# Retention's key and query products ahead of its value products, and where its rotations stand

## The chip, the core and the metric

The kernel runs on one core of a Trainium2 chip. Each engine works through a queue of its own in order: TensorE (PE) multiplies, VectorE (DVE), ScalarE (ACT) and GpSimd (POOL) do the elementwise work, SyncE (SP) issues nearly all DMAs. The metric is the time of one execution in device microseconds.

## What is computed

A trunk of two layers for 1024 tokens of width 1024. Layer 0 has two branches, a diagonal state-space layer with a gated output and multi-scale retention with 8 heads; layer 1 is a convolution module. The change lies in layer 0. Of the reference this matters:

```python
# state-space branch: y comes out of the scan
y = jax.nn.gelu(y)
y = y * jax.nn.sigmoid(y @ glu_w + glu_b)
# retention: 8 heads, keys and queries 64 wide, values 128 wide
q = rope(q, positions) * (RET_DK ** -0.5)
k = rope(k, positions)            # [x1*cos - x2*sin, x1*sin + x2*cos]
scores = einsum('bnihd,bnjhd->bnhij', qc, kc) * intra        # within a chunk
kv = einsum('bnjhd,jh,bnjhe->bnhde', kc, k_dec, vc)          # into the state
# the state is carried over the chunks with a decay; out = intra + q * state,
# then every head is normalised by its own mean and variance
```

## The kernel before

Every float32 product is made of three products of split operands: `wh` (or `xh`) is a cast on ACT, `wl` (or `xl`) the remainder, a subtraction on DVE or POOL. `wnext` hands out weights in the order of a list (`plan`) two ahead of use: a load on SP, a cast on ACT, a subtraction. `weight_low` makes remainders of layer 1's weights early and stores them in DRAM: load `lf`, cast `lh` on ACT, subtraction, store `lo`. 24 such lows are made in layer 0; the constants `K_LOWS`, `V_LOWS` and `H_LOWS` say how many in which stretch, the argument `bufs` how many buffers each tile has.

The keys and queries of all heads, and the values, are each made by seven products of quarter sums in place of eight (Strassen's scheme): `ret_values` runs the value products V in the order `V_ORDER`, then `ret_keys` the key and query products K in the order `K_ORDER`. One product is 48 matmuls of 128x128 by 128x512. The first of all, V2, stands in front of the last output of the scan (`s5_out(7)`). ACT and DVE bring the banks into the values `vt` or the accumulators `acc`. Meanwhile `y_pass` applies the Gelu, and `y_operands` loads and splits y as operands `yh`, `yl` of the gated product.

Then come the heads, in four pairs (`ret_heads`): transposed keys (`ktp`, decayed into `kt`), key by value (`kv`), on DVE the chain of states `S`, the scores (`sp`, masked into `sc` on DVE), the output (`ro`), per head mean and variance (`mv`), the inverse root (`rs`: a square root on ACT that needs a table load, a reciprocal on DVE), the normalised output (`on`), its transposes (`rt`). Between these PE runs the gated product `mm_glu` of `glu_ahead`: a `tanh` on ACT, then on DVE a product with `yg`, which POOL has made of two loads.

The rotation (`ret_turn`): for keys and for queries, swapped copies `kswp`, `qswp` come by DMA, POOL multiplies the raw tile and the swapped one by the tables `ropek` in eight instructions, DVE adds in four. Pair 0's raw tiles stay in SBUF; those of pairs 1 to 3 are stored in halves to `kq_d` and loaded again, raw and swapped, beside the heads of the pair before.

The order on each queue is made by a scheduler at build time; `issue_after` keeps an instruction behind another in that order.

Of the kernel before, what the change touches and what calls it, by code (L numbers as in the profile page):

```python
# [19 lines left out]
P = 128  # L20
# [23 lines left out]
V_ORDER = (2, 3, 1, 4, 5, 6, 7)  # L44
K_ORDER = (1, 6, 7, 2, 5, 3, 4)
# [14 lines left out]
class Trunk:  # L60
# [22 lines left out]
    def plan(self):  # L83
# [4 lines left out]
        seq += [(None, f"V{i}_{j}") for i in V_ORDER for j in range(2)]  # L88
        seq += [(None, f"K{i}_{j}") for i in K_ORDER for j in range(2)]
# [86 lines left out]
    def wload_quarter(self, name):  # L176
# [3 lines left out]
        e = self.nc.vector if g == "V" and (i in (1, 2, 6) or j) else self.nc.gpsimd  # L180
# [165 lines left out]
    def layer0_front(self, st):  # L346
# [170 lines left out]
        self.v2 = self.value_product(2, xs[0][4:], [self.bank(f"mm_v2_{b}", aux=b == 3) for b in range(4)])  # L517
# [429 lines left out]
    def retention(self, st):  # L947
# [6 lines left out]
        nc.sync.dma_start(self.rk[:], A["rope_k"])  # L954
        self.mask = r0.tile([P, NH, P], F32, name="retmask")
        nc.sync.dma_start(self.mask[:], A["ret_mask"])
        self.g128 = r0.tile([P, 4], F32, name="g128")
        nc.sync.dma_start(self.g128[:], A["ret_g128"])
        self.kdec = r0.tile([P, NH, 64], F32, name="kdec")
        nc.sync.dma_start(self.kdec[:], A["ret_kdec"])  # L960
        self.reps = r0.tile([P, NH], F32, name="reteps")
        nc.sync.dma_start(self.reps[:], A["ret_eps"])
# [25 lines left out]
    def ret_turn(self, pair, raws=None):  # L988

        nc, tab, q = self.nc, self.rk, self.rq  # L990
        cs = [slice(h * HALF, (h + 1) * HALF) for h in range(2)]
        made = []
        for i, nm in enumerate("kq"):
            if raws:
                raw = src = raws[i]
            else:
                raw, src = q.tile([P, T], F32, name=f"{nm}raw_{pair}", tag="raw", bufs=2), self.kq_d[pair, i]
                nc.sync.dma_start(raw[:], src)
            swp = q.tile([P, T], F32, name=f"{nm}swp_{pair}", tag="swp", bufs=2)
            for b in range(4):  # L1000
                o = b ^ 1
                nc.sync.dma_start(swp[32 * b:32 * b + 32, :], src[32 * o:32 * o + 32, :])
            for c in cs:
                nc.gpsimd.tensor_tensor(raw[:, c], raw[:, c], tab[:, 0, c], op=ALU.mult)
            for c in cs:
                self.last_turn = nc.gpsimd.tensor_tensor(swp[:, c], swp[:, c], tab[:, 1, c], op=ALU.mult)
            made.append((nm, raw, swp))

        def finish():
            outs, adds = [], []  # L1010
            for nm, raw, swp in made:
                o = self.r0.tile([P, T], F32, name=f"{nm}rot_{pair}", tag=f"{nm}rot", bufs=1)
                outs.append(o)
                adds.append([lambda c=c, o=o, raw=raw, swp=swp: nc.vector.tensor_tensor(o[:, c], raw[:, c], swp[:, c], op=ALU.add)
                             for c in cs])
# [830 lines left out]
```

## Time and profile before

| what | value |
| --- | --- |
| median of 3 runs | 1180.71 us (1177.71 to 1185.98) |
| the profiled execution | 1179.18 us |
| its span | 1177.4 us |
| mean granted TensorE clock | 0.997 |
| PE busy | 1155.9 us, 98% |
| DVE busy | 954.2 us, 81% |
| POOL busy | 718.3 us, 61% |
| ACT busy | 566.6 us, 48% |
| value and key products on PE | about 336 to 496 us |
| heads with the gated product | about 496 to 645 us |

The span runs from the profiled execution's first instruction to its last; 1.8 us lie around it. PE's matmuls are pipelined and their ends are modelled, so that a matmul of 128x512 reads 0.39 us where the next starts 0.227 us later. The clock is the same in all slices, so times of PE's groups can be carried over.

### The profile page before, as it was taken

To read this page: it belongs to the slowest core of one execution; us is meant where nothing else is said; L and a number is where in the kernel's file an instruction comes from. 1 tells how busy PE (TensorE), PEld (TensorE's weight loads), DVE (VectorE), ACT (ScalarE), POOL (GpSimd) and SP (SyncE) were. 2 spreads that over 40 slices of the span, in tenths; PEclk is the share of its full clock that TensorE was granted. 3 is DMA by queue.
4 is the path that set the end of the run, shared out by engine and by line. 5 is a ranking of instruction groups with operands and counts; after the bars stand their busy time and mean duration, and the time that the engine had idled before them with its cause. 6 is when DMAs were issued, how large, how long until landed. Compare 5 with 4: busy or idle time off the path is not lost.

```text
span 1177.4 us, 17601 instructions
## 1 busy us (share of the span) xinstructions
PE 1155.9 (98%) x6102; PEld 958.2 (81%) x6102; DVE 954.2 (81%) x1541; ACT 566.6 (48%) x855; POOL 718.3 (61%) x499
## 2 busy tenths in 40 slices
PE   9999999999999999998999999999999999999997
PEld 7888788788887888877888788888888888888877
DVE  6889989999725666676888999579999999999643
ACT  7212342332236756413224846467756578544662
POOL 2049999888841143686532053439894689977742
PEclk9999999999999999999999999999999999999999
DMA  9359579877799979997676879975448653366863
GB/s 342 109 166 326 193 271 320 269 272 273 249 308 334 366 249 313 361 300 255 209 237 238 308 249 305 344 255 187 161 161 297 221 181 133 126 192 232 277 250 139
DMA packets 142137, 293.74 MB, mean 249 GB/s; under 512 B 14048, under 2 KB 42976, under 8 KB 141920
## 3 DMA queue, kind: packets, MB, share of 16 engines
q1 hardware_dynamic: 140896, 288.43, 72.2%
q10 hardware_dynamic: 1152, 4.19, 0.9%
q8 instruction: 48, 0.79, 0.3%
q14 instruction: 41, 0.34, 0.1%
HBM read 210.32 MB, written 81.20 MB: 248 GB/s over the span
## 4 chain that ended last, share of the span: by engine, by line
PE 70%; DVE 12%; DMA 10%; issue 3%; ACT 2%; SPq 1%; POOL 1%; DVEq 0%; ACTq 0%; POOLq 0%
PE mm_g L279 5%; PE mm_g L278 5%; PE mm_g L277 5%; PE mm_w L279 4%; PE mm_w L278 4%; PE mm_w L277 4%; PE mm_k L1026 4%; PE mm_a L279 2%; PE mm_b L278 2%; PE mm_a L278 2%; PE mm_b L279 2%; PE mm_a L277 2%; PE mm_b L277 2%; PE mm_oc L279 2%; PE mm_oc L278 2%
## 5 line engine op out<-in xcount | busy, mean ns | idle before, releaser
L1533 DVE SCALAR_TENSOR_TENSOR cv<-u,convw,cv 128x512 f32<-128x512 f32 x358 | 244.5, 748 | 4.5 <-ACT cv L1519 3.0
L1513 POOL TENSOR_TENSOR tp<-tp,tp 128x512 f32<-128x512 f32 x104 | 138.9, 1338 | 28.8 <-ACT tp L1512 23.5
L279 PE MATMUL mm_g<-xh,wl_g 128*128 128x512 f32 x256 | 100.8, 394 | 0.0
L278 PE MATMUL mm_g<-xl,wh_g 128*128 128x512 f32 x256 | 100.6, 393 | 0.0
L277 PE MATMUL mm_g<-xh,wh_g 128*128 128x512 f32 x256 | 100.4, 392 | 0.0
L1512 ACT ACTIVATE tp<-u,convw 128x512 f32<-128x512 f32 x104 | 69.8, 714 | 11.3 <-POOL tp L1513 11.0
L167 POOL TENSOR_TENSOR wl_K<-wf_K,wh_K 128x1024 fp32r<-128x1024 f32 x14 | 34.0, 2430 | 48.6 <-ACT wh_K L166 46.6
L278 PEld LDWEIGHTS mm_g<-xl,wh_g 128*128 128x128 f32 x256 | 48.1, 188 | 11.3 <-issue 1.6
L279 PEld LDWEIGHTS mm_g<-xh,wl_g 128*128 128x128 f32 x256 | 48.0, 188 | 10.5
L277 PEld LDWEIGHTS mm_g<-xh,wh_g 128*128 128x128 f32 x256 | 48.1, 188 | 9.6
L279 PE MATMUL mm_oc<-zh,wl_woc 128*128 128x512 f32 (+1 forms) x152 | 54.4, 359 | 0.6 <-DMA wl_woc<-lo_woc 0.6
L277 PE MATMUL mm_oc<-zh,wh_woc 128*128 128x512 f32 (+1 forms) x152 | 54.3, 361 | 0.0
L278 PE MATMUL mm_oc<-zl,wh_woc 128*128 128x512 f32 (+1 forms) x152 | 54.0, 356 | 0.0
L277 PE MATMUL mm_glu<-yh,wh_glu 128*128 128x512 f32 x128 | 51.2, 400 | 2.2 <-ACT yh L1270 2.2
L278 PE MATMUL mm_u<-xl,wh_u 128*128 128x512 f32 x128 | 50.0, 391 | 1.0 <-DVE xl L399 1.0
L278 PE MATMUL mm_glu<-yl,wh_glu 128*128 128x512 f32 x128 | 50.5, 394 | 0.2 <-DVE yl L1272 0.2
L279 PE MATMUL mm_glu<-yh,wl_glu 128*128 128x512 f32 x128 | 50.6, 396 | 0.0
L277 PE MATMUL mm_g<-h1h,wh_cg 128*128 128x512 f32 x128 | 50.3, 393 | 0.0
L277 PE MATMUL mm_a<-h1h,wh_ca 128*128 128x512 f32 x128 | 50.2, 392 | 0.0
L279 PE MATMUL mm_b<-h1h,wl_cb 128*128 128x512 f32 x128 | 50.2, 392 | 0.0
L279 PE MATMUL mm_a<-h1h,wl_ca 128*128 128x512 f32 x128 | 50.0, 390 | 0.0
L279 PE MATMUL mm_g<-h1h,wl_cg 128*128 128x512 f32 x128 | 49.8, 389 | 0.0
(834 smaller groups left out, 3671.9 us busy)
## 6 DMA issues: line engine op xcount, KB each, us to landing
wf_g<-w_ab SPq DMA_DIRECT2D x16, 512.0 KB, 6.2
a<-w_out SPq DMA_DIRECT2D x32, 256.0 KB, 4.5
ws<-a SPq DMA_DIRECT2D x32, 256.0 KB, 4.5
lf<-w_c SPq DMA_DIRECT2D x32, 256.0 KB, 5.1
wf_p<-ws SPq DMA_DIRECT2D x16, 512.0 KB, 4.8
wf_cb<-w_c SPq DMA_DIRECT2D x16, 512.0 KB, 5.0
wf_ca<-w_c SPq DMA_DIRECT2D x16, 512.0 KB, 4.8
wl_cb<-lo_cb SPq DMA_DIRECT2D x16, 512.0 KB, 3.3
```

Of the source, the lines that this page charges most:

```text
L167: e.tensor_tensor(wl[:].rearrange(fl), wf[:], wh[:].rearrange(fl).bitcast(F32), op=ALU.subtract)
L277: nc.tensor.matmul(ps, wh[:, kb, :], xh, start=start, stop=False, skip_group_check=chain)
L278: nc.tensor.matmul(ps, wh[:, kb, :], xl, start=False, stop=False, skip_group_check=chain)
L279: self.last_mm = nc.tensor.matmul(ps, wl[:, kb, :], xh, start=False, stop=stop, skip_group_check=chain)
L1026: self.last_mm = self.nc.tensor.matmul(ps, l[:, k, :], r[:], start=start and k == m == 0, stop=stop and k == 3 and m == 2, skip_group_chec ...
L1512: nc.scalar.mul(sk[:], u[:, k:k + HALF], cw[:, nb, k:k + 1])
L1513: gp.tensor_tensor(s0[:], s0[:], sk[:], op=ALU.add)
L1533: v.scalar_tensor_tensor(dst[:], *tap, accs_[i][:], op0=ALU.mult, op1=ALU.add)
```

## The change

The key products now run first: K2 takes V2's place in front of `s5_out(7)`, then the other six, then all seven value products. ACT copies and DVE adds the key products into accumulators; those of pairs 2 and 3 lie in the space of half the values. `turn` rotates in place, with swaps from SBUF to SBUF. Pair 2 and pair 0 (`TURNS`) are rotated during the values' sweep, pair 1 beside the heads of pair 0, pair 3 beside those of pair 2. Pair 2 (rotated) and pair 3 (raw) are stored and come back into the tiles of pairs 0 and 1 when these are done. All remainders of key and value weights are made on DVE. Of the 24 lows, 6 stand in the key sweep, 8 in the value sweep and 10 in the heads (before: 6 beside the values, 14 beside the keys, 4 in the heads). The y operands of the first half are made after V7, the second half after V5 and V3, and the gated product takes the first half first. Three weights of the projection after the heads are loaded behind the last load of `ys_d`. The core of the diff:

```diff
--- before.py
+++ after.py
-LOWS, K_LOWS, V_LOWS, H_LOWS = 24, 20, 6, (0, 2, 4, 4)
+LOWS, K_LOWS, V_LOWS, H_LOWS = 24, 6, 14, (0, 4, 8, 10)
 NG = 4
+TURNS = (2, 0)
...
-V_ORDER = (2, 3, 1, 4, 5, 6, 7)
-K_ORDER = (1, 6, 7, 2, 5, 3, 4)
+K_ORDER = (2, 3, 1, 4, 5, 6, 7)
+V_ORDER = (1, 6, 2, 7, 5, 3, 4)
...
-        self.nc.sync.dma_start(wf[:], src if len(src.shape) == 2 else src.rearrange("p k n -> p (k n)"))
+        with self.tc.issue_after(self.ys_loaded.ins) if name in ("p1_3", "p2_0", "p2_1") else nullcontext():
+            self.nc.sync.dma_start(wf[:], src if len(src.shape) == 2 else src.rearrange("p k n -> p (k n)"))
...
-        e = self.nc.vector if g == "V" and (i in (1, 2, 6) or j) else self.nc.gpsimd
+        e = self.nc.vector if True else self.nc.gpsimd
...
-        self.v2 = self.value_product(2, xs[0][4:], [self.bank(f"mm_v2_{b}", aux=b == 3) for b in range(4)])
+        self.k2 = self.key_product(2, xs[0][4:], [self.bank(f"mm_k2_{b}", aux=b == 3) for b in range(4)])
         self.s5_out(7)
...
+            self.ret_keys(vp)
             V = self.ret_values(vp)
-            raws = self.ret_keys(vp)
...
-        done = 0
-        cur = self.ret_turn(0, raws)
         self.glu_ahead(0)
         for pair in range(4):
-            K, Q, qadds = cur()
+            K, Q = self.kq[pair]
             with self.tc.issue_after((self.last_rs if pair else self.last_turn).ins):
-                for k in range(K_LOWS + H_LOWS[pair], K_LOWS + H_LOWS[pair + 1]) if pair < 3 else ():
+                for k in range(V_LOWS + H_LOWS[pair], V_LOWS + H_LOWS[pair + 1]) if pair < 3 else ():
                     self.weight_low(ry, k, (("la", "lb"), ("la", "lb")), 1, nc.gpsimd)
 
             def turned():
+                if pair in (0, 2) and pair + 1 not in TURNS:
+                    with self.tc.issue_after(self.last_kt.ins), self.tc.issue_after(self.last_yg.ins):
+                        self.turn(pair + 1)
...
-            if pair < 3:
-                cur = self.ret_turn(pair + 1)
-            self.ret_heads(pair, K, Q, qadds, V, turned)
+            self.ret_heads(pair, K, Q, V, turned)
+            if pair in (0, 1):
+                pl, tags, bufs = self.kq_home[pair]
+                self.kq[pair + 2] = [pl.tile([P, T], F32, name=f"{nm}rot_{pair + 2}", tag=t, bufs=bufs) for nm, t in zip("kq", tags)]
+                self.acc[pair + 2] = [t[:] for t in self.kq[pair + 2]]
+                for q in range(2):
+                    nc.sync.dma_start(self.kq[pair + 2][q][:], self.kq_d[pair + 2, q])
             if pair < NG - 1:
                 self.glu_ahead(pair + 1)
...
+    def turn(self, pair):
+
+        nc, tab = self.nc, self.rk
         cs = [slice(h * HALF, (h + 1) * HALF) for h in range(2)]
         for i, nm in enumerate("kq"):
+            raw = self.acc[pair][i]
+            swp = self.rq.tile([P, T], F32, name=f"{nm}swp_{pair}", tag="swp", bufs=2)
             for b in range(4):
                 o = b ^ 1
+                nc.sync.dma_start(swp[32 * b:32 * b + 32, :], raw[32 * o:32 * o + 32, :])
             for c in cs:
                 nc.gpsimd.tensor_tensor(raw[:, c], raw[:, c], tab[:, 0, c], op=ALU.mult)
             for c in cs:
+                nc.gpsimd.tensor_tensor(swp[:, c], swp[:, c], tab[:, 1, c], op=ALU.mult)
+            for c in cs:
+                self.last_turn = nc.vector.tensor_tensor(raw[:, c], raw[:, c], swp[:, c], op=ALU.add)
+            if pair > 1 and pair in TURNS:
+                nc.sync.dma_start(self.kq_d[pair, i], raw)
...
+    def key_product(self, i, xs, pss):
+
+        for j in range(2):
+            w = self.wnext(f"K{i}_{j}")
+            for b in (2 * j, 2 * j + 1):
+                self.part(pss[b][:], w, b, xs, start=i not in (6, 7), stop=True, chain=i in (1, 6, 7))
+        return pss
...
+        self.kq_home = [(self.rq, ("raw", "raw"), 2), (self.r0, ("krot", "qrot"), 1)]
+        self.kq = [[pl.tile([P, T], F32, name=f"{nm}rot_{p}", tag=t, bufs=bufs) for nm, t in zip("kq", tags)]
+                   for p, (pl, tags, bufs) in enumerate(self.kq_home)] + [None, None]
+        acc = self.acc = [[t[:] for t in self.kq[p]] for p in range(2)]
+        acc += [[self.vt[1][h][:, 2 * q:2 * q + 2, :].rearrange("p a n -> p (a n)") for q in range(2)] for h in range(2)]
...
+                for q, h in {2: ((0, 0),), 3: ((0, 1),), 4: ((1, 0),), 5: ((1, 1),)}.get(i, ()):
+                    self.last_copy = nc.scalar.copy(acc[b][q][:, h * HALF:(h + 1) * HALF], ps[:])
+                for q, h in {1: ((0, 0),), 5: ((0, 1),), 6: ((0, 1),), 7: ((1, 0), (1, 1))}.get(i, ()):
+                    c = slice(h * HALF, (h + 1) * HALF)
+                    self.last_add = v.tensor_tensor(acc[b][q][:, c], ps[:], acc[b][q][:, c], op=ALU.add)
...
+            pss = self.value_product(i, xs[i], held if i in (6, 7) else ps4)
+            if n == 0:
+                for p in range(2, 4):
+                    if p not in TURNS:
+                        for q in range(2):
+                            nc.sync.dma_start(self.kq_d[p, q], self.acc[p][q])
+            if n < len(TURNS):
+                self.turn(TURNS[n])
...
+            for h, kbs in {7: ((0, range(KB)),), 5: ((1, range(4)),), 3: ((1, range(4, KB)),)}.get(i, ()):
+                self.y_operands(vp, h, kbs)
...
-        for h in (0, 1) if nb else (1, 0):
+        for h in range(2):
...
-        with self.tc.issue_after(self.last_kt.ins):
-            for add in qadds:
-                add()
         turned()
```

How the queues stand before and now, at the three places of which the prediction speaks.

On DVE, in pair 0's heads, before, behind the transposed keys: pair 0's own query adds, two gated results, then the states `S` and the masks in a row; pair 1's key adds (`krot<-kraw,kswp`) come last.

```order
L1014 TENSOR_TENSOR qrot_4980<-qacc_4169,qswp_4898 128x512 x2
L1095 SCALAR_TENSOR_TENSOR yg_1_4913<-mm_glu_1_4918,yg_1_4913 128x512
L1095 SCALAR_TENSOR_TENSOR yg_0_4946<-mm_glu_0_4951,yg_0_4946 128x512
L1195 COPY S_5034<-kv_0_5035 128x128
L1197 SCALAR_TENSOR_TENSOR S_5034<-S_5034,g_3591,kv_0_5035 128x128 x3
L1197 SCALAR_TENSOR_TENSOR S_5034<-S_5034,g_3591,kv_0_5048 128x128 x2
L1210 TENSOR_TENSOR sc_0_5058<-sp_0_5060,retmask 128x512
L1197 SCALAR_TENSOR_TENSOR S_5034<-S_5034,g_3591,kv_0_5048 128x128
L1210 TENSOR_TENSOR sc_0_5059<-sp_0_5061,retmask 128x512
L1210 TENSOR_TENSOR sc_0_5058<-sp_0_5072,retmask 128x512
L1210 TENSOR_TENSOR sc_0_5059<-sp_0_5073,retmask 128x512
L1014 TENSOR_TENSOR krot_5292<-kraw_4997,kswp_4999 128x512 x2
```

Now: pair 1's adds (`krot_3597`, `qrot_3598`) stand between the transposed keys and the states, and within the states.

```order
L1169 TENSOR_TENSOR kt_4973<-ktp_0_4974,kdec 128x512
L1097 SCALAR_TENSOR_TENSOR yg_0_4881<-mm_glu_0_4886,yg_0_4881 128x512
L1169 TENSOR_TENSOR kt_4973<-ktp_0_4980,kdec 128x512
L1004 TENSOR_TENSOR krot_3597<-krot_3597,kswp_4986 128x512 x2
L1191 COPY S_5008<-kv_0_5009 128x128
L1097 SCALAR_TENSOR_TENSOR yg_1_4914<-mm_glu_1_4919,yg_1_4914 128x512
L1193 SCALAR_TENSOR_TENSOR S_5008<-S_5008,g_3589,kv_0_5009 128x128 x3
L1004 TENSOR_TENSOR qrot_3598<-qrot_3598,qswp_4997 128x512
L1193 SCALAR_TENSOR_TENSOR S_5008<-S_5008,g_3589,kv_0_5022 128x128
L1004 TENSOR_TENSOR qrot_3598<-qrot_3598,qswp_4997 128x512
L1193 SCALAR_TENSOR_TENSOR S_5008<-S_5008,g_3589,kv_0_5022 128x128 x2
L1206 TENSOR_TENSOR sc_0_5032<-sp_0_5034,retmask 128x512
```

What moved: four adds of the next pair, each of which waits for POOL, from behind the masks to between the links of `S`, on which the `ro` products wait.

On POOL, at the same place, before (the third gated weight's remainder, half of pair 1's rotation, two `yg`, a remainder, the first low):

```order
L269 TENSOR_TENSOR wl_glu_4909<-wf_glu_4907,wh_glu_4908 128x1024
L1004 TENSOR_TENSOR kraw_4997<-kraw_4997,ropek 128x512 x2
L1006 TENSOR_TENSOR kswp_4999<-kswp_4999,ropek 128x512 x2
L1091 TENSOR_TENSOR yg_1_4913<-yg_1_4913,yn_1_4915 128x512
L1091 TENSOR_TENSOR yg_0_4946<-yg_0_4946,yn_0_4948 128x512
L269 TENSOR_TENSOR wl_glu_5222<-wf_glu_5220,wh_glu_5221 128x1024
L234 TENSOR_TENSOR lh_4984<-lf_4983,lh_4984 128x512
L1004 TENSOR_TENSOR qraw_5008<-qraw_5008,ropek 128x512 x2
```

Now:

```order
L270 TENSOR_TENSOR wl_glu_4877<-wf_glu_4875,wh_glu_4876 128x1024
L1093 TENSOR_TENSOR yg_0_4881<-yg_0_4881,yn_0_4883 128x512
L1093 TENSOR_TENSOR yg_1_4914<-yg_1_4914,yn_1_4916 128x512
L1000 TENSOR_TENSOR krot_3597<-krot_3597,ropek 128x512 x2
L1002 TENSOR_TENSOR kswp_4986<-kswp_4986,ropek 128x512 x2
L1000 TENSOR_TENSOR qrot_3598<-qrot_3598,ropek 128x512 x2
L1002 TENSOR_TENSOR qswp_4997<-qswp_4997,ropek 128x512 x2
L235 TENSOR_TENSOR lh_4948<-lf_4947,lh_4948 128x512
```

What moved: all eight multiplications of pair 1's rotation (`x2` are two) stand behind the two `yg` products and ahead of the first low's subtraction.

On ACT, from the gated results of the second block to the square roots of pair 1, before:

```order
L1094 ACTIVATE mm_glu_1_5264<-mm_glu_1_5264,hgb 128x512
L1094 ACTIVATE mm_glu_0_5542<-mm_glu_0_5542,hgb 128x512
L233 CAST lh_5303<-lf_5302 128x512
L268 CAST wh_glu_5831<-wf_glu_5830 128x1024
L1094 ACTIVATE mm_glu_1_5575<-mm_glu_1_5575,hgb 128x512
L563 ACT_TABLE_LOAD
L563 ACTIVATE rs_0_5425<-mv_0_5416,reteps 128x4
L563 ACTIVATE rs_0_5443<-mv_0_5434,reteps 128x4
```

Now:

```order
L1096 ACTIVATE mm_glu_1_5242<-mm_glu_1_5242,hgb 128x512
L234 CAST lh_5271<-lf_5270 128x512
L1096 ACTIVATE mm_glu_0_5510<-mm_glu_0_5510,hgb 128x512
L234 CAST lh_5277<-lf_5276 128x512
L269 CAST wh_glu_5805<-wf_glu_5804 128x1024
L1096 ACTIVATE mm_glu_1_5543<-mm_glu_1_5543,hgb 128x512
L234 CAST lh_5283<-lf_5282 128x512
L234 CAST lh_5290<-lf_5289 128x512
L564 ACT_TABLE_LOAD
L564 ACTIVATE rs_0_5389<-mv_0_5380,reteps 128x4
L564 ACTIVATE rs_0_5407<-mv_0_5398,reteps 128x4
```

What moved: where one low's cast (`lh`) stood behind the `tanh` of pair 1's blocks and ahead of the table load for `rs`, there are four, each between or behind two `tanh`.

More of the change, by code (lines that the diff above doesn't have):

```diff
@@ L1005, in ret_turn @@
             for c in cs:
[L1006 to L1015, printed above, removed]
-            for add in adds[0]:
-                add()
-            return outs[0], outs[1], adds[1]
-        return finish
+                nc.gpsimd.tensor_tensor(swp[:, c], swp[:, c], tab[:, 1, c], op=ALU.mult)
[3 more added lines that the diff above has]
+                nc.sync.dma_start(self.kq_d[pair, i], raw)
     def part(self, ps, w, b, xs, start=False, stop=False, chain=False):
@@ L1106, in value_product @@
                     xh, xl = xs[2 * j + k]
-                    first, last = j == k == 0 and i not in (6, 7), j == k == 1
+                    first, last = j == k == 0 and i not in (6, 7, 3), j == k == 1
                     nc.tensor.matmul(pss[b][:], xh[:, o], wh[:, k, :], start=first, stop=False, skip_group_check=chain)
@@ L1132, in summed @@
             return v.scalar_tensor_tensor(o, ps, r, o, op0=ALU.mult, op1=ALU.add)
-        self.fetch = fetch
-        x12 = self.x12 = self.xs[1][:4]
-        spare = self.spare = [tuple(vp.tile([P, HALF], F32R, name=f"xt{q}{kb}") for q in "hl") for kb in range(4)]
-        xs = self.xq = {1: self.xs[0][:4], 2: self.xs[0][4:], 3: self.xs[1][4:], 4: fetch(4, x12), 5: fetch(1, spare)}
+        xs, self.ys_in, pss = self.xq, [[], []], {}
         for n, i in enumerate(V_ORDER):
+            if i in (1, 2, 5, 4):
+                ps4 = [self.bank(f"mm_v{i}_{b}", aux=i in (2, 5) or b == 3) for b in range(4)]
@@ L1139, in ret_values @@
             if i == 1:
-                held = pss = [self.bank(f"mm_v{i}_{b}") for b in range(4)]
-            elif i != 2:
-                pss = held if i in (6, 7) else [self.bank(f"mm_v{i}_{b}", aux=b == 3) for b in range(4)]
-            pss = self.v2 if i == 2 else self.value_product(i, xs[i], pss)
-            if i in (4, 5):
-                xs[{4: 6, 5: 7}[i]] = fetch(*{4: (2, x12), 5: (3, spare)}[i])
+                held = ps4
+            pss = self.value_product(i, xs[i], held if i in (6, 7) else ps4)
```

120 lines of the change are left out of this document (46 added, 74 removed).

## The prediction

> **What bounds the kernel now.** I read four views: the page's first two parts, the list of what TensorE (PE) waited for, the timelines of all engines around the heads of retention (496 to 650 us), and the groups by tile for the tiles that move. First the page (the second line is the span in 40 slices of 29.4 us).
>
> ```profile
> PE 1155.9 (98%) x6102; PEld 958.2 (81%) x6102; DVE 954.2 (81%) x1541; ACT 566.6 (48%) x855; POOL 718.3 (61%) x499
> DVE  6889989999725666676888999579999999999643
> ```
>
> PE is busy 98% of 1177.4 us and the change alters no matmul count, so only PE's waits can be gained, or new ones made. Here are those that lie in the changed stretch.
>
> ```profile
> PE rt L1260 <- DVE mv L1247: 2.4, 1, 2.4
> PE mm_glu L277 <- ACT yh L1270: 2.2, 1, 2.2
> PE rt L1260 <- DVE on L1252: 2.1, 2, 1.2
> PE mm_v L1108 <- ACT wh_V L166: 1.4, 1, 1.4
> ...
> PE kv L1187 <- DVE kt L1170: 1.0, 1, 1.0
> ...
> PE mm_glu L278 <- DVE yl L1272: 0.2, 1, 0.2
> ```
>
> Together 9.3 us: all that can be gained, under 1% of the time. After the heads PE waits for nothing worth 1 us, so a wait made or removed here moves the end one for one. What makes such a wait is seen in pair 0's heads. (Start, length, then the instruction; in brackets the idle time before it and what ended it.)
>
> ```profile
> 496.13 0.39 PE L277 MATMUL mm_glu<-yh,wh_glu 128*128 128x512 f32 x1
> 531.66 0.62 ACT L233 CAST lh<-lf 128x512 fp32r<-128x512 f32 x1 [9.88 <-DMA lf<-w_c]
> 532.30 1.28 ACT L563 ACT_TABLE_LOAD   x1
> 533.60 0.30 ACT L563 ACTIVATE rs<-mv,reteps 128x4 f32<-128x4 f32 x1
> 537.78 1.06 PE L1260 MATMUL rt<-ident,on 128*128 128x128 f32 x8 [2.37 <-DVE mv L1247]
> 539.81 0.61 ACT L233 CAST lh<-lf 128x512 fp32r<-128x512 f32 x1
> 547.99 0.62 ACT L233 CAST lh<-lf 128x512 fp32r<-128x512 f32 x1 [4.07 <-DMA lf<-w_c]
> 570.54 1.03 PE L1260 MATMUL rt<-ident,on 128*128 128x128 f32 x8
> ```
>
> The 2.37 us before pair 0's transposes (rt) are named after DVE, but ACT is late: its queue held a weight low's cast (lh) that waited 9.88 us for a load, and the square root (rs) stood behind it. From rs to rt passes 4.2 us (537.78 less 533.60). The lows share one buffer each way, so a low takes a whole cycle of load, cast, subtraction and store; the casts are 8.15 us apart (531.66, 539.81, 547.99). I call 496.13, the first gated matmul, T. Pair 1's transposes leave at T+74.4.
>
> **What is taken away.** If none of the six waits came back, 9.3 us go. For the 1.4 (wh_V behind the Gelus) I accept it: the key product's casts stand ahead of the Gelus on ACT now. For the 2.1 and 1.0 of pairs 2 and 3 too: 24 gated matmuls now lie between the two sets of transposes and 27 between the transposed keys and their product, where before nothing did, and at 0.227 us each (13 steps from 541.22 to 544.17) they are 5.4 and 6.1 us of cover.
>
> ```profile
> 541.22 0.39 PE L279 MATMUL mm_glu<-yh,wl_glu 128*128 128x512 f32 x1
> ...
> 544.17 0.39 PE L277 MATMUL mm_glu<-yh,wh_glu 128*128 128x512 f32 x1
> ```
>
> **The key and value sweeps.** Fourteen low parts of key weights go from POOL to DVE, with the value ones that POOL had.
>
> ```profile
> L167 POOL TENSOR_TENSOR wl_K<-wf_K,wh_K x14: 2392/2404/2721, 409.3 to 484.1; 128x1024 fp32r<-128x1024 f32 x14
> L167 DVE TENSOR_TENSOR wl_V<-wf_V,wh_V x10: 1208/1224/1696, 307.8 to 405.4; 128x1024 fp32r<-128x1024 f32 x10
> ```
>
> POOL loses 34 us and DVE takes 17, in slices where DVE is 5 to 6 tenths busy; each stands on DVE at least 4 us ahead of its first matmul, also where a rotation's add stands before it (pair 2's key adds are through early in the first value product). Cost 0; without that cover 1.2 us for each. The evictions of the seven key products move to ACT and DVE in the same number. One spot is tight: a bank of the second product waits for a copy that stands behind the landing of the last y_d store, by my walk free 1.6 us before PE needs it. I take 0, bound 1.5. The stores and loads of raw pairs fall from 18 to 8, which no PE wait names: 0. The projection's weights p1_3 are issued after the last ys load, some 17 us later, still 8 us ahead of their first matmul: 0.
>
> **Pair 1's rotation beside pair 0's heads.** This is the first large term. On POOL its eight multiplications now stand behind the third gated weight's low part and the two yg products; on DVE its four adds stand *inside* pair 0's state chain (S), and DVE works in order, so S, the masks and every product of S with the queries queue behind POOL.
>
> ```profile
> 507.98 0.62 ACT L1270 CAST yh<-yf 128x512 fp32r<-128x512 f32 x1 [5.40 <-DMA yf<-yn_d]
> 497.15 1.05 ACT L268 CAST wh_glu<-wf_glu 128x1024 fp32r<-128x1024 f32 x1
> 507.34 2.35 POOL L269 TENSOR_TENSOR wl_glu<-wf_glu,wh_glu 128x1024 fp32r<-128x1024 f32 x1
> 512.58 2.99 POOL L1006 TENSOR_TENSOR kswp<-kswp,ropek 128x512 f32<-128x512 f32 x2
> 515.53 2.97 POOL L1091 TENSOR_TENSOR yg<-yg,yn 128x512 f32<-128x512 f32 x2
> 501.10 3.37 POOL L1004 TENSOR_TENSOR qacc<-qacc,ropek 128x512 f32<-128x512 f32 x2 [0.64 <-DVE krot L1014]
> 528.23 2.52 POOL L1006 TENSOR_TENSOR qswp<-qswp,ropek 128x512 f32<-128x512 f32 x2 [0.18 <-issue]
> 521.92 0.34 DVE L1197 SCALAR_TENSOR_TENSOR S<-S,g,kv 128x128 f32<-128x128 f32 x1
> 523.16 0.27 PE L1232 MATMUL ro<-S,qrot 64*128 64x128 f32 x1
> ```
>
> The last y operand's cast came at T+11.9 before. It is now one product earlier in the program, but the loads still pass through three buffers of 5.4 us and a cast and a split each, so I put it at T+11.2 and the product's wait at 1 us in place of 2.4. Then in order: that cast 0.6, wh_glu 1.05, wl_glu 2.4, two yg 2.7, four pairs of rotation at 2.5 to 3.0, say 11: T+29.0. One DVE add of 0.7 and two S of 0.34: T+30.4. PE was at its first ro at T+27.0 (523.16), with 2.4 us of waits and 78 gated matmuls before it; now there are 68, so with the 1 us it is there at T+23.3. The wait is **7.1 us**; with rotations of 2.5 and a last cast 2 us earlier 4, with rotations of 3.4 about 10. The Trainium skill's page GPSIMD Engine Reference, section 1, Specifications, says that GpSimd shares its SBUF interfaces with VectorE and collides with its two-input instructions, which speaks against a rotation beside DVE's heads; the pairs here between 2.52 and 2.99 us agree with it, and by it the upper figures would hold.
>
> **Ten lows in the heads instead of four.** The second large term. H_LOWS puts four lows after pair 0's start, four after its last rs, two after pair 1's; still one buffer, subtracted by POOL. On ACT, pair 1's square root now stands behind the eighth. Low 1's subtraction stands behind the rotation on POOL: T+30.3. SP issues its store and then load 2: T+31.1.
>
> ```profile
> DMA to landing us min/median/max: 2.8/5.1/7.5
> ```
>
> Landed after 5.1 and cast: T+36.8. Six more cycles of 8.15 as measured: low 8 is cast at T+85.7. Table load 1.28 and 4.2 to the transposes: T+91.2. On the way the same queue holds pair 1's keys (their eviction stands on DVE behind a yg that waits for a tanh behind low 5: T+64.8, where PE could be at about 57) and its state (a yg behind low 6). These are inside the T+91.2, not added. Before, these transposes left at T+74.4: **+16.8 us**, the 7.1 in place of the old 2.4, 2.2, 0.9 and 0.2 included. Bounds: a landing of 2.8 makes a cycle of 5.4 (0.62 cast, 1.29 subtraction, 0.7 issue), low 8 comes at T+66.9, and PE's own T+68.7 (74.4 less waits of 5.7) plus 7.1 decides: +1.4. A landing of 6.5 makes 9.1 and T+98: +24. I take the measured cycle: same tiles, same buffers, same engines.
>
> **Pair 3's rotation beside pair 2's heads.** It is loaded raw, swapped in SBUF, turned, and its adds stand before pair 2's state on DVE.
>
> ```profile
> qraw<-kq_d SPq DMA_DIRECT2D x3, 512.0 KB, 7.9
> qswp<-kq_d SPq DMA_DIRECT2D x12, 128.0 KB, 7.8
> ```
>
> The query half: load 7.9, swap 7.8, rotation 5.0, add 1.4, state 2, one after the other. SP issues the load behind low 8's store, about T+88.5, so the state is there at T+112.6. From T+91.2 PE has 55 gated matmuls (12.5) and some 6 us of keys and scores: T+110. I take 2.5 us, bounds 0 and 9.
>
> **Sum.** 16.8 + 2.5, less 1.4 (wh_V), less 1.2 and 1.0 (second rt wait of pair 2, kv of pair 3): +15.7. On the profiled execution of 1179.18 (span 1177.4 and 1.8 around it) that is **1194.9 us**; against the median 1180.71 of the runs, which is 1.5 above the profiled one, +1.2%. 1% is about what a measurement of this kernel can tell from no change, since its three runs lie 0.7% apart.
>
> **Rivals.** (a) *The lows' loads land quickly* and their casts hold nothing. For it: the last low landed in about 2.9 us (its cast is at 547.99); against: its median is 5.1. Then 1.4 + 2.5 - 3.6: 1179.5. The skill's DMA: Bandwidth & Descriptors, section Anatomy of one DMA, fits 2.0 us plus bytes over 436 GB/s (measured on GpSimd's path); by it 256 KB would take an estimated 2.6 us and this rival would hold, but the trace's median of 5.1 contradicts it. (b) *The rotation is not in the way*: if the last y operand comes at T+3, POOL is through 8 us earlier, S waits for nothing and the lows start 8 us earlier: pair 1's transposes at T+83.2, +8.8, in all 1179.2 + 8.8 + 2.5 - 3.6 = 1186.9. Against: three buffers. (c) *Faster*: neither queue binds, all 9.3 us go: 1169.9. For it: no key or value product waits for DMA; against: pair 0's cast, which cost 2.4 us with only four lows. (d) *Pair 3's chain decides as well*: SP's queue holds its loads one low longer (8 us): 1194.9 + 6.5 = 1201.4, up to 1208. For it: 14 loads and swaps of it stand between stores that wait; against: PE then is late too.
>
> **Chances.** Forecast 0.52, (a) 0.18, (b) 0.09, (c) 0.05, (d) 0.16. Of the forecast's share three quarters lie over 1% (1192.5), with all of (d): slower 0.55. Faster by over 1% needs under 1168.9, thus more than (c): 0.03. Within 1%: 0.42. The range 1179 to 1208 reaches from (a) to the end of (d).
>
> **What would show it.** In the profile after: PE's waits headed by ro or S of pair 0 (5 to 11 us, behind POOL's rotation), rt of pair 1 behind lh and rs, with kv of pair 1 between; ten lh on POOL about 8 us apart; wh_V gone from the list. If the lows come 5 to 6 us apart, or ro of pair 0 waits under 3 us, I am wrong on that term. If the sweeps show waits of over 2 us, I missed one.

## The result, and the profile after

The changed kernel takes 1198.75 us (median of 5 runs, 1197.17 to 1199.80), the one before 1180.42 on the same chip (5 runs, 1177.71 to 1185.98): ratio 1.0153, 95% interval 1.0134 to 1.0171. It is slower by 1.5%. The profiled execution has a span of 1198.0 us, 20.6 more than before. What PE waited for, longest first (total, times, longest):

```profile
PE mm_w L278 <- ACT ysh L1293: 8.9, 1, 8.9
PE rt L1256 <- DVE mv L1243: 3.2, 1, 3.2
PE sp L1200 <- DVE S L1193: 3.0, 2, 1.9
PE ro L1228 <- DVE S L1193: 2.6, 1, 2.6
PE mm_w L280 <- DVE wl_p L168: 2.6, 1, 2.6
PE mm_v L1110 <- DVE v L1126: 2.2, 1, 2.2
```

Of the six waits shown before, those of wh_V, of the second transposes of pair 2, of kv and of yh and yl are gone. One is new and larger than any of them: the first product of the output projection (mm_w) waits 8.9 us for the split row block ysh. The timeline around it, PE, SP's issues and ACT:

```profile
649.27 1.03 PE L1256 MATMUL rt<-ident,on 128*128 128x128 f32 x8
650.63 0.92 SPq L1262 DMA_DIRECT2D yr_d<-grl  x2
654.58 0.80 SPq L1298 DMA_DIRECT2D yr<-yr_d  x2
655.42 0.43 SPq L1307 DMA_DIRECT2D t2f<-ys_d  x1
659.45 0.63 ACT L1293 ACTIVATE ysh<-t2f 128x512 fp32r<-128x512 f32 x1 [2.27 <-DMA t2f<-ys_d]
660.13 1.65 PE L278 MATMUL mm_w<-ysh,wh_p 128*128 128x512 f32 x3 [8.90 <-ACT ysh L1293]
```

From pair 3's last transposes to that product it takes 10.9 us: product with the gate, store, load of the gated rows (t2f), split. Before it took 13.4, and PE waited for nothing in between, since 55 of the 384 gated matmuls came behind those transposes. The two ends before:

```profile
631.73 1.03 PE L1260 MATMUL rt<-ident,on 128*128 128x128 f32 x8
645.09 0.62 PE L277 MATMUL mm_w<-ysh,wh_p 128*128 128x512 f32 x2
```

Now 380 gated matmuls stand ahead of the last transposes and 4 behind (counted in PE's order).

A second thing is seen in the granted clock. From 330 us to 1174 it is 0.50 in six stretches of the changed kernel and in one of the kernel before (last line), and 1.00 outside them (us; PE, PEld, DVE, ACT, POOL busy; granted clock; DMA):

```profile
474.44:477.84 3.40, 3.40 (x10) 2.62 (x9) 2.51 (x4) 0.59 (x2) 0.00 (x0) 0.50 0.90 301
522.23:525.62 3.39, 3.39 (x15) 2.32 (x15) 2.05 (x4) 0.34 (x1) 3.39 (x3) 0.50 0.88 239
573.43:576.82 3.39, 3.39 (x14) 2.90 (x12) 3.25 (x17) 1.30 (x4) 0.00 (x0) 0.50 0.78 201
597.32:600.72 3.40, 3.40 (x20) 3.18 (x17) 1.85 (x6) 0.00 (x0) 0.00 (x0) 0.50 1.01 356
655.35:665.57 10.22, 5.44 (x12) 3.93 (x13) 7.44 (x11) 4.68 (x8) 1.46 (x1) 0.50 0.96 325
754.34:757.73 3.39, 3.39 (x10) 2.62 (x9) 3.39 (x3) 2.15 (x4) 2.88 (x2) 0.50 0.83 219
508.71:512.10 3.39, 3.17 (x10) 2.29 (x11) 1.86 (x2) 1.38 (x2) 3.39 (x3) 0.50 0.75 222
```

Across the large wait the clock falls at 655.3 and stays at 0.50 until 665.6: matmuls of 512 columns start every 0.427 us there, and every 0.227 afterwards. A wait of this length is paid for twice.

**Where the 20.6 us are.** The span of each kernel's profiled execution, cut at the same events (us; *ratio* is the time against before on the same chip, with its 95% interval; *sweeps* from the first key or value product to the first gated matmul, *heads* to the last transposes, *gap* to the first mm_w):

| run | median | ratio | ahead | sweeps | heads | gap | rest |
|---|---|---|---|---|---|---|---|
| before | 1180.4 |  | 336.3 | 159.8 | 135.6 | 13.4 | 532.3 |
| changed | 1198.8 | 1.0153 (1.0134-1.0171) | 335.0 | 162.6 | 151.6 | 10.9 | 537.9 |
| ys_early | 1204.2 | 1.0215 (1.0188-1.0242) | 334.9 | 159.6 | 150.9 | 15.2 | 538.7 |
| weights_free | 1196.5 | 1.0147 (1.0128-1.0167) | 334.0 | 160.8 | 153.4 | 13.2 | 533.1 |
| lows_in_sweep | 1189.8 | 1.0100 (1.0071-1.0129) | 334.3 | 160.4 | 145.1 | 11.1 | 536.6 |
| lows_on_dve | 1200.2 | 1.0166 (1.0137-1.0195) | 335.7 | 161.2 | 156.4 | 10.8 | 534.7 |
| turn1_in_sweep | 1194.7 | 1.0139 (1.0116-1.0162) | 336.1 | 166.3 | 141.6 | 10.7 | 534.7 |
| gated_first | 1194.1 | 1.0121 (1.0098-1.0144) | 335.5 | 160.1 | 151.7 | 3.4 | 540.5 |
| gated_lows | 1185.7 | 1.0057 (1.0033-1.0081) | 335.2 | 160.1 | 146.7 | 3.4 | 538.4 |
| gated_lows_turn1 | 1186.5 | 1.0055 (1.0034-1.0077) | 336.0 | 166.4 | 139.2 | 3.4 | 540.2 |
| all_three | 1186.4 | 1.0060 (1.0041-1.0079) | 334.1 | 159.9 | 147.1 | 3.4 | 540.9 |
| no_lows_in_heads | 1192.0 | 1.0107 (1.0079-1.0135) | 333.9 | 160.5 | 152.0 | 2.1 | 541.4 |
| turn1_lows_early | 1187.2 | 1.0072 (1.0045-1.0098) | 334.9 | 168.4 | 137.3 | 3.4 | 541.0 |
| turns_in_sweep | 1190.5 | 1.0099 (1.0067-1.0132) | 332.8 | 171.7 | 138.6 | 1.9 | 541.6 |

Heads and gap together are 13.5 us longer. The waits there are 17.7 (8.9, 3.2, 3.0, 2.6) in place of 7.9 (2.4, 2.2, 2.1, 1.0, 0.2): 9.8. In the heads the clock is 0.50 for 10.2 us in place of 3.4; at half clock at most half of the time is lost, so at most 3.4 more. These two leave some 0.3. The rest is 5.6 longer: the wait for wl_p at 753 us (2.6, before 0.5) and at most 4.4 lost at half clock (5.4 us at 0.50 behind the 8.9, 3.4 behind that wait). The sweeps lose 2.8: a wait of 2.2 for a bank where the 1.4 of wh_V stood, and at most 1.7 of half clock behind it. What lies ahead of the sweeps gives 1.3 back.

Each row is one execution. What lies ahead of the sweeps is the same work in all thirteen changed versions and takes 332.8 to 336.1 us there, and sweeps with the same lows and rotations take 159.6 to 162.6. So a difference of up to 3 us in one column is not shown by one row; the waits and the clock behind it are.

### The profile page after: what moved, and what is told of

The parts are those of the page before. It is cut to its first block, busy times and chain, and to the rows that moved or that the text cites. A ratio compares the mean times of both kernels' runs of the same rounds, so it can differ in the third digit from the quotient of the medians.

```text
span 1198.0 us, 17558 instructions
## 1 busy us (share of the span) xinstructions
PE 1164.4 (97%) x6102; PEld 965.6 (81%) x6102; DVE 957.7 (80%) x1545; ACT 571.2 (48%) x863; POOL 691.0 (58%) x487
## 4 chain that ended last, share of the span: by engine, by line
PE 67%; DVE 11%; DMA 11%; issue 5%; POOL 3%; ACT 2%; SPq 1%; DVEq 0%; POOLq 0%; ACTq 0%
PE mm_k L1013 6%; PE mm_g L280 6%; PE mm_g L279 6%; PE mm_g L278 5%; PE mm_w L278 3%; PE mm_w L279 3%; PE mm_w L280 3%; PE mm_a L280 2%; PE mm_a L278 2%; PE mm_b L280 2%; PE mm_b L278 2%; PE mm_b L279 2%; PE mm_a L279 2%; PE mm_oc L280 2%; PE mm_oc L279 2%
## 5 line engine op out<-in xcount | busy, mean ns | idle before, releaser
L234 ACT CAST lh<-lf 128x512 fp32r<-128x512 f32 x32 | 19.9, 621 | 93.0 <-DMA lf<-w_c 92.8
L279 PEld LDWEIGHTS mm_g<-xl,wh_g 128*128 128x128 f32 x256 | 48.1, 188 | 11.2 <-issue 1.6
L1000 POOL TENSOR_TENSOR v<-v,ropek 128x512 f32<-128x512 f32 x4 | 6.1, 1540 | 84.2 <-DMA kswp<-v 78.1
```

The lines of the kernel that those rows point to most:

```text
L234: self.nc.scalar.copy(hi[:], f[:])
L279: nc.tensor.matmul(ps, wh[:, kb, :], xl, start=False, stop=False, skip_group_check=chain)
```

## The experiments

Medians and ratios as in the table. The runs were on other chips, where the kernel before took 1177.6 to 1180.0 us and not 1180.4. So the ratios compare versions better than the times do, and two versions whose intervals overlap widely are not told apart.

**ys_early.** The theory first read from the trace: the gated rows' loads are late because of their place in SP's queue.

```diff
-                self.ys_loaded = nc.sync.dma_start(sg[:], self.ys_d[rows(nb), hs(h)])
+                self.ys_loaded = nc.gpsimd.dma_start(sg[:], self.ys_d[rows(nb), hs(h)])
```

> The changed kernel with one thing else: the eight loads of the gated rows 0 to 3 from DRAM (t2f and t3f from ys_d, L1307) are issued by POOL behind its product yg of block (6,1), not by SP behind the two stores of pair 3's output (yr_d) and the loads yr that wait for them. Theory A (the order on SP makes the wait of 8.9 us in front of the first w_out product): these loads land some 15 us before they are needed, the wait of mm_w for ysh falls from 8.9 to 1 to 5 us (what is left is the tanh of the last gated blocks, which stands on ACT at 654.0 to 657.2 behind a table load), and the time is 1191 to 1195. Rival B (the wait belongs to pair 3's late transposes, whose result the w_out products need anyway): the wait moves to the products that read yr0, and the time stays at 1197 to 1200.

Measured 1204.24 us (1201.03 to 1206.62; 1.0215 of before, 1.0188 to 1.0242): slower than the changed kernel and than both theories said. Theory A is wrong. POOL's issue and what then stands ahead of the split on ACT:

```profile
650.09 0.71 POOL L1307 DMA_DIRECT2D t2f<-ys_d  x1 [19.33 <-DVE wl_p L168]
659.44 0.62 ACT L1266 CAST yr00h<-yr0f 128x512 fp32r<-128x512 f32 x1 [6.67 <-DMA yr0f<-yr_d]
659.96 0.62 ACT L1293 ACTIVATE ysh<-t2f 128x512 fp32r<-128x512 f32 x1
```

POOL was free for 19.3 us and still could not issue the load. The row names the DVE instruction that ended last before it, but the program's own semaphores say what was waited for: t2f_0 waits for DVE's last product into grl_7 and for stores to land, since the tiles t2f_0, t3f_0, t2f_1 and t3f_1 lie on the addresses of pair 3's tiles grl_7 and grl_6. On SP that wait was hidden in the order, since the store and a load behind it stood ahead. So whatever needs row 0 comes a store and a load behind the last transposes. The new queue made another order on ACT, where the split now stands behind the cast of a later load: 4.3 us more. Other tiles for these rows were not tried: beside the stage's other tiles 1.9 KB per partition are left, less than one tile.

**weights_free.**

```diff
-        with self.tc.issue_after(self.ys_loaded.ins) if name in ("p1_3", "p2_0", "p2_1") else nullcontext():
+        with nullcontext():
```

> The changed kernel without the one condition that holds the loads of the w_out weights p1_3, p2_0 and p2_1 back until the ys rows are loaded. Theory A (the loads of ys_d stand behind the stores of yr_d on SP, whatever the weights do): the wait of 8.9 us stays within 1 us and the time is 1197 to 1200. Rival W (the late weights are what the w_out products wait for): the time falls by 3 us or more, to 1190 to 1196.

Measured 1196.48 (1194.60 to 1196.78): between the two, 2.3 less than the changed kernel, but against before the ratio is 1.0147 for 1.0153, which is no difference. The wait for ysh grew to 11.2 and the one for wl_p at 753 went; the table's rest is 4.8 us shorter and heads and gap some 4 longer. So the condition is not the cause of the large wait, and that it is worth anything in all is not shown.

**lows_in_sweep.**

```diff
-LOWS, K_LOWS, V_LOWS, H_LOWS = 24, 6, 14, (0, 4, 8, 10)
+LOWS, K_LOWS, V_LOWS, H_LOWS = 24, 8, 20, (0, 2, 4, 4)
```

> The changed kernel with its lows placed as before in the heads: four of them beside the heads (0, 2, 2, 0 per pair) instead of ten, the other six in the two sweeps (8 of 24 in the keys', 20 by the end of the values'). Theory P (the prediction's largest term: ten lows on ACT and POOL delay the transposes of pair 1): pair 1's transposes come 8 us or more earlier and the time falls to 1185 to 1191. Theory T (read from the trace after: the lows ran in 7.0 us each and pair 1's transposes were only 1.6 us later than before, so the lows hardly cost anything): 1196 to 1200, and the wait in front of the first w_out product stays at 8 to 10 us, since the transposes of pair 3 still stand behind 380 of the 384 gated matmuls.

Measured 1189.82 (1187.75 to 1194.62), 8.9 less, some 6 by the ratios: theory P's time. T's time is wrong, though the last wait stays as T said. The heads are 6.5 us shorter, by fewer waits and by the clock (0.50 for 3.4 us of them in place of 10.2). The sweeps are no longer although they hold six lows more. What PE still waits for:

```profile
PE mm_w L278 <- ACT ysh L1293: 9.2, 1, 9.2
PE mm_w L280 <- DVE wl_p L168: 2.6, 2, 1.7
PE sp L1200 <- DVE S L1193: 2.0, 1, 2.0
PE mm_v L1110 <- DVE v L1126: 1.7, 1, 1.7
PE rt L1256 <- DVE mv L1243: 1.2, 1, 1.2
```

Pair 1's transposes leave 69.9 us behind the first gated matmul instead of 75.5, 5.6 earlier and not the 8 of P.

**lows_on_dve.**

```diff
-                    self.weight_low(ry, k, (("la", "lb"), ("la", "lb")), 1, nc.gpsimd)
+                    self.weight_low(ry, k, (("la", "lb"), ("la", "lb")), 1, nc.vector)
```

> The changed kernel with the subtraction of the ten lows beside the heads on DVE instead of POOL; their loads, casts and stores stay. It asks by what the ten lows cost 7 us in the heads (lows_in_sweep). Theory Q (by POOL: its queue holds yg and wl_glu back, and DVE's two-input operations are slowed while it works): the transposes of pair 1 come 3 us or more earlier and the time is 1190 to 1195. Rival D (by the casts on ACT and the load and store each low waits for, or 0.7 us more of DVE inside the heads' chains): 1197 to 1202.

Measured 1200.20 (1195.24 to 1201.54): rival D, though the ratio, 1.0166, is not clear of the changed kernel's. The heads are 4.8 us longer. A subtraction on DVE waits for its cast, and what comes behind it waits too; the clock is at 0.50 for 17.1 us of the heads in place of 10.2. One such row, and the wait for the state S (6.9 in two, 3.0 in the changed kernel):

```profile
565.17 0.69 DVE L235 TENSOR_TENSOR lh<-lf,lh 128x512 fp32r<-128x512 f32 x1 [6.25 <-ACT lh L234]
PE sp L1200 <- DVE S L1193: 6.9, 2, 3.8
```

So DVE is no better place than POOL. The lows' loads and casts on ACT are the same in both; what of their cost is these and what is POOL's queue, the runs don't separate.

**turn1_in_sweep.**

```diff
-TURNS = (2, 0)
+TURNS = (2, 0, 1)
```

> The changed kernel with the rotation of pair 1 also in the values' sweep (behind the third of its seven products), so that only pair 3's stands beside the heads. Theory R (the rotation's additions on DVE inside pair 0's chain, and its products on POOL, make the waits of 3.0 and 2.6 us in front of pair 0's scores and outputs): these two fall below 1.5 us together and the time is 1192 to 1196. Rival S (the sweep has no room: rotation, splits and evictions on DVE come late there): the waits of mm_v grow from 2.2 by as much as the heads win, and the time is 1197 to 1202.

Measured 1194.72 (1191.21 to 1195.78): theory R's time, but the ratio, 1.0139, is not clear of the changed kernel's. Pair 0's waits for S are gone and the heads are 10.0 us shorter, but rival S is right too: the sweeps are 3.7 longer than the changed kernel's, 5 to 7 longer than those of the other runs with two rotations there. First two of DVE's splits, one while POOL turns and one when it is done; then what PE waits for:

```profile
449.48 2.31 DVE L168 TENSOR_TENSOR wl_V<-wf_V,wh_V 128x1024 fp32r<-128x1024 f32 x1
450.67 3.99 POOL L1002 TENSOR_TENSOR qswp<-qswp,ropek 128x512 f32<-128x512 f32 x2
476.07 1.21 DVE L168 TENSOR_TENSOR wl_V<-wf_V,wh_V 128x1024 fp32r<-128x1024 f32 x1
478.09 0.77 PE L1110 MATMUL mm_v<-wh_V,xh 128*128 128x512 f32 x1 [3.92 <-DVE v L1126]
```

The same split takes 2.31 us beside POOL's product and 1.21 without it. At 474.2 DVE is still behind: an add of the rotation, a low, a y split and that wl_V stand ahead of the eviction v (477.20), for whose bank the sixth product waits. How much of this is the slower splits and how much the adds themselves, the runs don't separate.

**gated_first.** After ys_early the order of the sum is changed, not the load: the four row blocks that need no load come first.

```diff
-BLOCKS = ((4, 0), (4, 1), (0, 0), (0, 1), (1, 0), (1, 1), (5, 0), (5, 1), (2, 0), (2, 1), (3, 0), (3, 1), (6, 0), (7, 0), (6, 1), (7, 1))
+BLOCKS = ((4, 0), (4, 1), (5, 0), (5, 1), (6, 0), (7, 0), (0, 0), (0, 1), (1, 0), (1, 1), (2, 0), (2, 1), (3, 0), (3, 1), (6, 1), (7, 1))
...
-        for kb in range(KB):
-            self.mm3(ps, w, kb, (xs[kb][0][:], xs[kb][1][:]), first and kb == 0, kb == KB - 1, True)
+        for n, kb in enumerate((4, 5, 6, 7, 0, 1, 2, 3) if first else range(KB)):
+            self.mm3(ps, w, kb, (xs[kb][0][:], xs[kb][1][:]), first and n == 0, n == KB - 1, True)
```

> The changed kernel with another order in front of the w_out products: of the eight row blocks that the first four products sum, the four that were gated late (4 to 7, never stored) come first, and the four that are loaded from ys_d last; the loads and splits of rows 0 to 3 stand behind those of rows 4 to 7 in the code. Theory C (after ys_early: the tiles t2f_0, t3f_0, t2f_1, t3f_1 lie in the memory of pair 3's tiles grl, so their loads wait for its last products and stores wherever they are issued, and everything that needs row 0 begins 11 us behind the last transposes): the first products begin on row 4 some 5 to 7 us earlier, with 36 matmuls (8 us) to cover the loads, and the time is 1190 to 1194. Rival B (what follows needs pair 3's output as late anyway): the wait moves to the products that read rows 0 to 3 or yr0, and the time stays at 1196 to 1200.

Measured 1194.14 (1192.31 to 1195.29), 4.6 less, some 4 by the ratios, whose intervals just overlap: theory C, 0.1 over its upper end. The first product comes 3.4 us behind the last transposes instead of 10.9; 2.6 of the gain are lost again in the rest:

```profile
650.72 0.98 PE L278 MATMUL mm_w<-ysh,wh_p 128*128 128x512 f32 x3 [1.48 <-ACT ysh L1293]
659.70 0.62 ACT L1266 CAST yr00h<-yr0f 128x512 fp32r<-128x512 f32 x1 [4.83 <-DMA yr0f<-yr_d]
660.22 0.62 ACT L1293 ACTIVATE ysh<-sg 128x512 fp32r<-128x512 f32 x1
660.90 0.96 PE L278 MATMUL mm_w<-ysh,wh_p 128*128 128x512 f32 x3 [2.50 <-ACT ysh L1293]
```

Row 7's split, whose data are long there, stands on ACT behind the cast of a load that lands at 659.7.

**gated_lows**: gated_first and lows_in_sweep together.

> gated_first and lows_in_sweep together. Theory C with the lows' own cost: the two gains are at different places (the heads, and the wait behind them) and add up: 1189.8 less 5 to 7 is 1182 to 1186. Rival: with the lows gone from the heads the scheduler puts the gated products elsewhere and the tail wait is not shortened: 1188 to 1191.

Measured 1185.70 (1183.37 to 1190.94; 1.0057 of before, 1.0033 to 1.0081): the gains add, 13.1 us in all (11 by the ratios). With the next two it is the fastest version; the runs don't tell these three apart. In the table its sweeps are those of before, heads and gap 1.1 longer. What is left is in the rest: PE waits four times for operands of the output projection between 646 and 670 us, 4.2 us together, and the clock is at 0.50 from 647.2 to 650.6.

**gated_lows_turn1**: with `TURNS = (2, 0, 1)` too.

> gated_lows with pair 1's rotation in the values' sweep as well. If the gains add (turn1_in_sweep had 10 us less between the first gated matmul and the first w_out product than the changed kernel, and lost 6 of them in the sweep; lows_in_sweep had 6 less): 1178 to 1183, no slower than before. Rival (the sweep is full: 20 lows and three rotations on DVE and POOL there, where a subtraction on DVE takes 1.78 in place of 0.68 us while POOL works): mm_v and wl_V waits reach 8 us or more, and the time is 1185 to 1190.

Measured 1186.51 (1184.57 to 1187.26): the rival's time, with waits of 5.5 us (mm_v 4.8, wl_V 0.7) for its 8. The heads win 7.5 us, the sweeps lose 6.3, the rest 1.8.

**all_three**: gated_lows and weights_free together.

> gated_lows without the condition that holds the w_out weights p1_3, p2_0 and p2_1 back. In gated_lows the fourth product then waits 1.2 us for wh_p (ACT) and 1.7 for wl_p (DVE), 667.39 and 669.65. Theory W: with the wait for ysh out of the way these late weights are the next thing that is late, and the time falls by 2 to 4 us to 1181 to 1184. Rival: the earlier weights take DMA and ACT from the loads and splits of the ys rows, as in weights_free (wait 11.2 in place of 8.9): 1185 to 1189.

Measured 1186.44 (1183.89 to 1187.93): the rival's time; its reason is not shown. The waits in the fourth product are still there:

```profile
PE mm_w L278 <- ACT wh_p L167: 2.0, 1, 2.0
PE mm_w L280 <- DVE wl_p L168: 1.3, 1, 1.3
```

**no_lows_in_heads**: all_three with `24, 8, 24, (0, 0, 0, 0)`.

> all_three with no low beside the heads (8 in the keys' sweep, 16 in the values'). If the lows cost in proportion (ten cost 7 to 9 us against four), the last four are worth 3 to 5 us: 1177 to 1181, as long as the values' sweep holds 16; rival: the sweep is full, mm_v waits 3 us or more longer, and the time is 1183 to 1188.

Measured 1191.96 (1189.69 to 1194.30): slower than either said. The sweep is no longer (160.5), but its last lows reach into pair 0, where DVE waits for a cast and the transposed keys (kt) queue behind. The wait of 4.57 is paid for twice as well: the clock is at 0.50 from 516.0 to 529.7.

```profile
515.48 0.69 DVE L235 TENSOR_TENSOR lh<-lf,lh 128x512 fp32r<-128x512 f32 x1 [3.21 <-ACT lh L234]
516.82 3.26 PE L1183 MATMUL kv<-v,kt 128*64 128x128 f32 x28 [4.57 <-DVE kt L1169]
```

**turn1_lows_early**: all_three with `TURNS = (2, 0, 1)` and `24, 12, 20, (0, 2, 4, 4)`.

> all_three with pair 1's rotation in the values' sweep, and four more of the lows in the last two products of the keys' (12 there, 8 in the values'). It asks whether the 4.8 us of mm_v in gated_lows_turn1 come from the count of DVE operations in the sweep. Theory F (DVE is full there, lows and rotation alike): with four lows fewer mm_v waits under 2.5 us, and the time is 1178 to 1182. Rival: the wait stays at 4 to 5 us, since the eviction stands behind the splits of the y rows and of wl_V, which are as before: 1182 to 1186.

Measured 1187.18 (1185.44 to 1190.35): the rival's reading, 1 us over its range. With four lows fewer in the values' sweep the wait is longer, not shorter, so it does not hang on their count.

```profile
478.02 0.76 PE L1110 MATMUL mm_v<-wh_V,xh 128*128 128x512 f32 x1 [6.28 <-DVE v L1126]
```

**turns_in_sweep**: turn1_lows_early with `TURNS = (2, 3, 0, 1)`.

> turn1_lows_early with pair 3's rotation in the values' sweep too (all four there, in the order 2, 3, 0, 1). It asks what pair 3's rotation beside pair 2's heads costs (the prediction's term of +2.5) and what the sweep takes. Term right and room in the sweep: the waits of pair 2's scores for S (1.4 us) go, and the time is 1 to 3 us below turn1_lows_early. Rival: four rotations of some 11 us on POOL slow DVE in the sweep (a two-input operation takes 1.78 in place of 0.68 us there), mm_v and wl_V wait 4 to 10 us longer, and the time is 1186 to 1194.

Measured 1190.49 (1188.43 to 1195.04): the rival's time, but not its waits: mm_v and wl_V wait 7.9 us together, 1 more than before this change and not 4 to 10. No wait for S is left among the first rows, but heads and gap are only 0.2 us shorter than in turn1_lows_early (140.5 for 140.7), and the sweeps 3.3 longer:

```profile
PE mm_v L1110 <- DVE v L1126: 4.9, 1, 4.9
PE mm_w L278 <- ACT ysh L1293: 3.7, 2, 3.1
PE mm_v L1111 <- DVE wl_V L168: 3.0, 2, 2.3
```

No version here is faster than the kernel before.

## Why the prediction came out as it did

The total is right, 1194.9 within a range of 1179 to 1208 for 1198.75, and so is slower by over 1%. Its parts are not: one term was far too large, and two things were not in the sum. That these errors nearly cancelled is luck.

**Taken away.** The waits for wh_V, for pair 2's second transposes and for kv went as said. For the 1.4 of wh_V a wait of 2.2 came back in the values' sweep, where I had taken 0: the tight bank was not the key product's that I had walked through but the one in which the sixth value product adds to the fifth and must wait for its eviction.

**Pair 1's rotation, 7.1 us.** The place and the cause were right, the size half:

```profile
500.64 0.62 ACT L1266 CAST yh<-yf 128x512 fp32r<-128x512 f32 x1 [2.64 <-DMA yf<-yn_d]
508.18 2.52 POOL L1000 TENSOR_TENSOR krot<-krot,ropek 128x512 f32<-128x512 f32 x2
517.82 1.75 DVE L1004 TENSOR_TENSOR qrot<-qrot,qswp 128x512 f32<-128x512 f32 x1 [0.57 <-POOL qswp L1002]
522.04 0.59 PE L1228 MATMUL ro<-S,qrot 64*128 64x128 f32 x2 [2.62 <-DVE S L1193]
```

The first gated matmul, T, is 497.63 here. The last y operand was cast at T+3.0, not T+11.2: its three buffers did not hold it back. POOL's turn took 10.9 us (508.18 to 519.03) for my 11 and ended at T+21.4 instead of 29.0. PE waited 1.1 and 2.6 for S, 3.7 in all. That is rival (b)'s condition with a wait left over that (b) did not have. turn1_in_sweep shows that the term was real: without the rotation the heads are 10.0 us shorter, which is more than these waits; part of it is the clock, at 0.50 there for 3.4 us in place of 10.2. The 2.52 to 2.99 us that I gave for a pair on POOL left out one of 3.37 in my own rows; the four here took 10.9 together, so the upper figures did not hold.

**Ten lows, +16.8 us.** The term that failed. Pair 1's transposes left at T+75.5, 1.1 later than before. The mechanism is there, word for word:

```profile
525.28 0.62 ACT L234 CAST lh<-lf 128x512 fp32r<-128x512 f32 x1 [14.76 <-DMA lf<-w_c]
567.02 0.62 ACT L234 CAST lh<-lf 128x512 fp32r<-128x512 f32 x1 [8.43 <-DMA lf<-w_c]
567.66 1.28 ACT L564 ACT_TABLE_LOAD   x1
568.95 0.30 ACT L564 ACTIVATE rs<-mv,reteps 128x4 f32<-128x4 f32 x1
573.14 1.69 PE L1256 MATMUL rt<-ident,on 128*128 128x128 f32 x8 [3.23 <-DVE mv L1243]
```

The square root stands behind the eighth low's cast, and 4.2 us pass from it to the transposes, as before. But low 2 was cast at T+27.7 (predicted 36.8; the rotation ended 7.6 earlier) and the six cycles from there to low 8 took 6.96 us each, between 5.3 and 9.1, not 8.15. Three casts of one pair were too few to take a cycle from, and a chain of six multiplies the error. lows_in_sweep gives the size: six lows fewer shorten the heads by 6.5 us.

**Pair 3's rotation, +2.5.** One wait of 1.9 for S in pair 2: right in size. turns_in_sweep shows no gain beyond 0.2 us in heads and gap from taking it away once the lows are fewer.

By the prediction's own signs, too, ro of pair 0 waited under 3 us, two of the six cycles took 5 to 6, and the sweeps had a wait of over 2.

**Not in the sum: the cover's other end.** I counted 24 and 27 gated matmuls as new cover for pair 2's transposes and pair 3's keys, and did not ask where they had stood. They were the cover of the last transposes, whose store, load and split take 10.9 us. "After the heads PE waits for nothing worth 1 us" was true of the kernel before and no property of the place. This wait, 8.9 us, is the largest single one. gated_first shows that it hangs on the rows that must be stored and loaded; that the moved matmuls had covered it is read from the two traces, and no run puts them back.

**Not in the sum: half clock.** "A wait made or removed here moves the end one for one" is wrong. PE was busy at half clock for 22.4 us in place of 3.4 (the stretches above, without the wait itself), so up to 9.5 us more were lost by it: up to nearly half of the 20.6.

**The late weights, 0.** "Still 8 us ahead of their first matmul" spoke of their own first use only. weights_free shows the wait for wl_p at 753 that comes of it, but no difference in the time as a whole.

So a term 15.7 us too large (16.8 for 1.1) stood against 8.9 of a wait, up to 9.5 of half clock and some 2 of what I had at 0 or can't place: the bank, wl_p, small pieces.

## What to carry to other kernels

Filler work is a fixed stock: when a new order puts more of it in front of one wait, find the wait from which it was taken, above all the last one before a stage that can't start without a store and a load. Before a late load is moved to another queue, see which tile lay in its memory. A loop of load, cast and store beside a critical chain is dear by what stands behind its waits on an in-order queue (here the square root on ACT, or the state on DVE), so its place matters more than the engine that subtracts.

## What the runs showed of the hardware

A PE wait of about 2 us and more mostly brought half clock behind it. In the changed kernel the six stretches at 0.50 follow waits of 2.24, 2.62, 3.23, 1.92, 8.9 and 2.60 us. In the kernel before, one follows the wait of 2.2 for yh; the 2.37 us wait at 537.78 brought none (1.00 from 538 to 541), nor did weights_free's 2.3 in front of mm_v. All but one of the stretches last 3.4 us, and the one across the large wait lasts three times that. In the changed kernel they begin 14, 15, 7, 17 and 29 times 3.41 us after one another (474.44, 522.23, 573.43, 597.32, 655.35 and 754.34 above), so the clock changed on a fixed beat and not at the waits. The Trainium skill's page TensorE: Matmul & The Clock Gate, part 1, says that the array runs at half its clock after an idle window of about 3.4 us, that the window runs freely, and that a busy one of the same length lifts it. The 0.50, the 0.427 against 0.227 us steps, the lengths and the beat agree; but five of the waits here were shorter than such a window, so it need not be idle throughout. How much of it must be, these traces don't settle.

DVE's two-input operations took up to about 1.1 us longer while POOL multiplied: in turn1_in_sweep 2.31 for 1.21 with 128x1024, and in the same sweep 1.78 for 0.68 with 128x512. The masks, one input of which lies in a bank, were not slowed: in the changed kernel POOL worked beside ten of the 16, and all took 0.68 to 0.69 us. POOL's own pairs took 2.5 to 4.0 us. A rotation on POOL is therefore paid for on DVE as well.
